# Feed-forward part of a two-layer encoder: product sums accumulated in PSUM, the next chunk's first product moved forward, the middle convolution tap on another engine, and operand preparation of the down-projection ordered behind additions

## The chip, the cores and the metric

The kernel runs on one core of a Trainium2 chip. The metric is the time of one execution on the device, in microseconds (us). The core's engines are named as in the profile: PE multiplies matrices (PEld loads its weights), DVE, ACT and POOL work on vectors, and SP issues most of the DMAs. Each engine works through its own list of instructions in order; semaphores tie the lists together. Matmuls sum in PSUM banks; all other tiles lie in SBUF.

## The reference, cut to what matters

```python
D_MODEL, SEQ, DEPTH, D_FF, CONV_W = 1024, 1024, 2, 2816, 3

def reference(x, ..., ffn_norm, w_up, conv_w, conv_b, w_down):
    for l in range(DEPTH):
        ...
        x = x + mix @ w_out[l]
        hf = rms_norm(x, ffn_norm[l]) @ w_up[l]
        gate, val = hf[..., :D_FF], hf[..., D_FF:]
        gate = depthwise_conv(gate, conv_w[l], conv_b[l])
        x = x + (gelu(gate, approximate=False) * val) @ w_down[l]
    return x
```

The convolution runs over the tokens, with three taps and a bias for each of the 2816 channels. Everything is float32. What stands in the place of the first dots (attention in two forms and a recurrence) is not touched by the change.

## The kernel before

**Tiling.** Activations lie transposed: 128 channels on the partitions, 1024 tokens along the row. The up-projection takes 22 chunks f; a chunk makes 128 channels of the gate and 128 of the value, for all 1024 tokens. Each float32 operand is split in a high and a low part (ACT makes the high one, `split`, L1063; DVE the difference, L1064), and a product is summed from three matmul terms, so a k-step costs three matmuls of 128 by 128 by 512.

**Seven products.** Gate and value, each in two halves of the tokens, form a 2 by 2 block product over two halves of the input channels. It is done in seven block products instead of eight, named "11", "21", "T2", "T3", "T1", "T4" and "22". Each has 12 matmuls (L1114), so a chunk has 84 and a layer 1848. In `up` each product gets a PSUM bank of its own ("pa", "pt" or "pb"), and the shared sums are made on DVE: ACT copies the first product into u2 (L1127), then DVE adds banks into u2, u3, the two halves of g (gate) and of v (value), seven additions of 512 columns (L1121).

**The gate.** `gate` scales g by the row factors rbc of the normalization (POOL, L1154), starts t with the middle tap and the bias (POOL, L1155), adds the two outer taps (DVE, L1156 and L1157), applies gelu (ACT, L1158) and scales by rbc again (POOL, L1159). DVE multiplies t by v (L1144) and SP stores t to the DRAM tensor hid (L1145).

**Weights.** While a chunk's products run, `up_weights` prepares the next chunk's seven weight operands: SP loads rv and rg (L1051 and L1052, 512 KB each), POOL makes four sums of 512 columns in the tiles ws and ws3 (L1059), and each of the seven operands "wo" is split on ACT and DVE. The loads, the sum tile ws and the seven operands take their buffers from one pool of 10 (`NWEIGHT`). A tile that takes a buffer waits for the last user of the tile that held it.

**Down-projection.** Again seven block products, in four groups g = 0 to 3 over 11 steps m, 24 matmuls a step (L1287; some steps 12). `prep` loads a step's pieces (256 KB each), makes sums and differences on DVE and splits them (L1177 is the line of a helper, `tt`, for all of these, and for the additions of `evacuate` too). Two steps are prepared ahead (`DOWN_AHEAD`). The sums of a group stay in PSUM over its 11 steps; at the end of group 0 `evacuate` adds eight banks to the rows X (written X<-X,pa in the profile), and group 1 then takes the same banks.

**Order.** A scheduler lists each engine's instructions ahead of time, from the order in which the code is traced and from its own estimates. `tc.issue_after`, which the change brings in, makes it list what is traced within it behind the named instruction.

Of the kernel before, what the change touches and what calls it, by code (L numbers as in the profile page):

```python
# [12 lines left out]
AF = mybir.ActivationFunctionType  # L13
ALU = mybir.AluOpType
AX = mybir.AxisListType.X

P = 128
D = 1024
T = 1024
# [6 lines left out]
NFF = D_FF // P  # L26
# [67 lines left out]
class Trunk:  # L94
# [953 lines left out]
    def up_weights(self, l, f, eng):  # L1048
        nc = self.nc
        rg, rv = (self.wslot([P, KC, P], name="wraw") for _ in range(2))  # L1050
        nc.sync.dma_start(rv, self.i["w_u"][l, 2 * f + 1])  # L1051
        nc.sync.dma_start(rg, self.i["w_u"][l, 2 * f])  # L1052
        (a11, a12), (a21, a22) = (
            [r.rearrange("p k o -> p (k o)")[:, 512 * j : 512 * j + 512] for j in range(2)] for r in (rv, rg)
        )
        s = self.wslot([P, 2, 512], name="ws")

        def sub(out, a, b, op=ALU.subtract):
            eng.tensor_tensor(out, a, b, op=op)  # L1059

        def split(src):
            o = self.wslot([P, 2, 512], F32R, name="wo")
            nc.scalar.activation(o[:, 0], src, AF.Copy)  # L1063
            nc.vector.tensor_tensor(o[:, 1], src, o[:, 0], op=ALU.subtract)  # L1064
            return o

        yield split(a11)
        yield split(a12)
        sub(s[:, 0], a21, a22, ALU.add)
        sub(s[:, 1], s[:, 0], a11)  # L1070
        yield split(s[:, 1])
        d = self.half([P, 512], "ws3")
        sub(d, a11, a21)
        yield split(d)
        yield split(s[:, 0])
        yield split(a22)
        sub(s[:, 1], a12, s[:, 1])
        yield split(s[:, 1])
# [3 lines left out]

    def up(self, l, X, td, acc, H):
        nc = self.nc
        for name in ("21", "T3", "T1", "T4", "22"):
            for k in range(4):
                a, b, ga, gb = X[k], X[k + 4], self.gain(l, k), self.gain(l, k + 4)
                if name == "21":
                    o = self.split_x(b[:, :512], gb, self.xslot)
                elif name == "22":  # L1090
                    o = self.split_x(b[:, 512:], gb, self.slot)
                elif name == "T1":
                    o = self.split_x(td[k][:, 0], None, self.xslot, nc.gpsimd)
                elif name == "T3":
                    d = self.half([P, 512], "xt")
                    nc.scalar.activation(d, a[:, 512:], AF.Copy, scale=ga)
                    nc.vector.scalar_tensor_tensor(d, b[:, 512:], gb, d, op0=ALU.mult, op1=ALU.subtract)
                    o = self.split_x(d, None, self.xslot)
                else:
                    d = td[k][:, 1]  # L1100
                    nc.vector.scalar_tensor_tensor(d, b[:, :512], gb, d, op0=ALU.mult, op1=ALU.subtract)
                    o = self.split_x(d, None, self.xslot)
                self.B[name, k] = o
        rbc = None
        for f in range(NFF):
            ahead = self.up_weights(l, f + 1, nc.gpsimd) if f + 1 < NFF else iter(())
            ops, self.ops = self.ops, []

            def product(j, x, tag):
                ps = self.bank2([P, 512]) if tag == "pa" else self.bank1([P, 512], tag=tag)  # L1110
                for k in range(4):
                    for u, v in ((0, 0), (0, 1), (1, 0)):
                        st, mv = ops[j][:, u, k * P : (k + 1) * P], self.B[x, k][:, v]
                        nc.tensor.matmul(ps, st, mv, start=k + u + v == 0, stop=k == 3 and u == 1)  # L1114
                o = next(ahead, None)
                if o is not None:
                    self.ops.append(o)
                return ps

            def add(out, x, y):  # L1120
                nc.vector.tensor_tensor(out, x, y, op=ALU.add)  # L1121

            pu = self.slot([P, 2, 512], name="pu")
            u2, u3 = pu[:, 0], pu[:, 1]
            g, v = self.slot([P, T], name="g"), self.slot([P, T], name="v")
            p1 = product(0, "11", "pa")
            nc.scalar.activation(u2, p1, AF.Copy)  # L1127
            p2 = product(1, "21", "pb")
            add(v[:, :512], u2, p2)
            p6 = product(2, "T2", "pt")  # L1130
            add(u2, u2, p6)
            p7 = product(3, "T3", "pt")
            add(u3, u2, p7)
            if rbc is None:
                rbc = self.factors(acc)
            p5 = product(4, "T1", "pb")
            add(g[:, 512:], u3, p5)
            add(u2, u2, p5)
            p4 = product(5, "T4", "pt")
            add(g[:, :512], u3, p4)  # L1140
            p3 = product(6, "22", "pb")
            t = self.gate(l, f, g, rbc)
            add(v[:, 512:], u2, p3)
            nc.vector.tensor_tensor(t, t, v, op=ALU.mult)  # L1144
            nc.sync.dma_start(H[f], t)  # L1145

    def gate(self, l, f, g, rbc):

        nc = self.nc
        cw = PP_CW + (l * NFF + f) * 3  # L1150
        w = [self.pp[:, cw + j : cw + j + 1] for j in range(3)]
        cb = self.pp[:, PP_CB + l * NFF + f : PP_CB + l * NFF + f + 1]
        t = self.slot([P, T], name="t")
        nc.gpsimd.tensor_tensor(g, g, rbc, op=ALU.mult)  # L1154
        nc.gpsimd.tensor_scalar(t, g, w[1], cb, op0=ALU.mult, op1=ALU.add)  # L1155
        nc.vector.scalar_tensor_tensor(t[:, 1:], g[:, : T - 1], w[0], t[:, 1:], op0=ALU.mult, op1=ALU.add)  # L1156
        nc.vector.scalar_tensor_tensor(t[:, : T - 1], g[:, 1:], w[2], t[:, : T - 1], op0=ALU.mult, op1=ALU.add)  # L1157
        nc.scalar.activation(t, t, AF.Gelu)  # L1158
        nc.gpsimd.tensor_tensor(t, t, rbc, op=ALU.mult)  # L1159
        return t  # L1160
# [8 lines left out]
    def down(self, l, H, spill, out):  # L1169

        nc = self.nc
# [4 lines left out]
        def tt(out, a, b, op=ALU.subtract):  # L1176
            nc.vector.tensor_tensor(out, a, b, op=op)  # L1177

        def split2(src):

            hi, lo = (self.xslot([P, 2, 512], F32R, name="bw") for _ in range(2))
            nc.scalar.activation(hi, src, AF.Copy)
            tt(lo, src, hi)
            return (hi[:, 0], lo[:, 0]), (hi[:, 1], lo[:, 1])
# [4 lines left out]
        def prep(g, k, m):  # L1189
# [34 lines left out]
                return ops  # L1224
            return [None, split2(p)]

        def add(x, ps):
            tt(x, x, ps, ALU.add)

        def evacuate(g, j, c, ps):  # L1230
            x, y = X[c], X[4 + c]
# [32 lines left out]
        steps = [(g, k, m) for g in range(4) for m, k in enumerate(DOWN_ORDERS[g])]  # L1264
        ready, late, acc = [], [], [None, None]
        for i, (g, k, m) in enumerate(steps):
            while len(ready) < min(len(steps), i + 1 + DOWN_AHEAD):
                ready.append(prep(*steps[len(ready)]))
            if g < 2:
                residual(g, m)  # L1270
            if m == 0 and g == 0:
                acc[0] = [p[:, h] for p in [self.bank2([P, T]) for _ in range(2)] for h in (h0, h1)]
            if m == 0 and g != 1:
                acc[1] = [self.bank1([P, 512], tag=t) for t in ("pt", "pt", "pb", "pb")]
            late.append((m, ready[i]))
            ready[i] = None
            if n - DOWN_TAIL <= m < n - 1:
                continue
            for j in range(2):
                first = g if j and g > 1 else 0  # L1280
                for c in range(4):
                    for q, ops in late:
                        if ops[j] is None:
                            continue
                        a, b = ops[j]
                        for u, v in ((0, 0), (0, 1), (1, 0)):
                            nc.tensor.matmul(  # L1287
                                acc[j][c],
                                a[u][:, c * P : (c + 1) * P],
                                b[v],  # L1290
                                start=g == first and q + u + v == 0,
                                stop=q == n - 1 and u == 1,
                                skip_group_check=g > first,
                            )
                    if m == n - 1 and ops[j] is not None:
                        evacuate(g, j, c, acc[j][c])
            late = []
        return X

# [169 lines left out]
```

## Time and profile before

| what | value |
|---|---|
| median of 3 runs | 2880.6 us (2879.34 to 2884.51) |
| the profiled execution | 2879.85 us, of which the span is 2878.0 us |
| PE, DVE, ACT, POOL busy | 97%, 78%, 47%, 42% of the span |
| up-projection, layer 0 | 775.87 to 1228.3 us of the span |
| down-projection, layer 0 | 1228.3 to about 1466 us |
| up-projection, layer 1 | 2204.0 to 2654.9 us |
| down-projection, layer 1 | 2654.9 to 2878 us |

A row of a group in the profile names line, engine, operation, the tile written and those read, the shape, the count, the busy time with the mean of one, and the idle time ahead with what ended it. Rows of a timeline begin with the start in us and the length. Matmul rows last longer than the distance between two matmuls, since they overlap; the distance is what counts.

### The profile page before, as it was taken

The page shows a single profiled execution, that of the slowest core. Times are in us where ns is not written, and L with a number is a line of the kernel's source. Part 1 is how long each engine was busy: PE and PEld are TensorE (multiplying, and loading weights), DVE is VectorE, ACT ScalarE, POOL GpSimd, SP SyncE. Part 2 cuts the span into 40 slices and gives each one's busy share as a digit, 9 for nine tenths or more (in the row PEclk, how much of TensorE's full clock was granted, in tenths as well). Part 3 has the DMA queues.
Part 4 walks back from the last instruction along what each step waited for, and adds up shares of the span by engine and source line. Part 5 has one row for each costly group of instructions (what it writes and reads, how often), then busy time and mean ns, then how long its engine had stood idle before and what let it go on. Part 6 is the DMA issues. An engine that isn't in the chain of part 4 may idle for free.

```text
span 2878.0 us, 40091 instructions
## 1 busy us (share of the span) xinstructions
PE 2782.9 (97%) x14984; PEld 2346.7 (82%) x14984; DVE 2253.6 (78%) x3044; ACT 1338.6 (47%) x2273; POOL 1214.2 (42%) x811
## 2 busy tenths in 40 slices
PE   8999999999999999999999999999999999999999
PEld 7999987777878777778899999877777777877787
DVE  5849668897778888896848495788967888888975
ACT  5526367786432222234535264677854222222332
POOL 2516545432366666510015265354323566665000
PEclk9999999999999999999999999999999999999999
DMA  4213262101312222474313033521012222225641
GB/s 148 83 34 101 73 161 70 45 16 46 115 59 87 82 74 87 140 281 140 118 54 85 25 108 85 137 70 45 15 66 95 79 82 74 84 83 196 234 157 66
DMA packets 155202, 273.63 MB, mean 95 GB/s; under 512 B 16768, under 2 KB 74368, under 8 KB 155008
## 3 DMA queue, kind: packets, MB, share of 16 engines
q1 hardware_dynamic: 145216, 241.71, 26.0%
q0 software_dynamic: 9792, 29.36, 3.8%
q8 instruction: 118, 1.93, 0.3%
q14 instruction: 76, 0.62, 0.1%
HBM read 201.80 MB, written 69.21 MB: 94 GB/s over the span
## 4 chain that ended last, share of the span: by engine, by line
PE 56%; DVE 16%; POOL 11%; DMA 7%; issue 6%; ACT 5%; SPq 0%; ACTq 0%; POOLq 0%; DVEq 0%
PE pa L269 10%; PE pa L281 10%; POOL ws L1059 6%; DVE wo L1064 6%; PE pa L1287 6%; DMA wraw<-w_u 5%; PE pb L860 5%; PE pa L774 5%; PE pb L1287 4%; PE pt L1287 4%; PE pt L845 3%; POOL t L1159 3%; ACT wo L1063 2%; PE pt L619 1%; PE pb L619 1%
## 5 line engine op out<-in xcount | busy, mean ns | idle before, releaser
L1114 PE MATMUL pt<-bo,wo 128*128 128x512 f32 x1584 | 392.3, 400 | 30.1 <-DVE pu L1121 24.2
L1114 PEld LDWEIGHTS pt<-bo,wo 128*128 128x128 f32 x1584 | 299.8, 192 | 113.0 <-issue 27.3
L1114 PE MATMUL pb<-bo,wo 128*128 128x512 f32 x1584 | 382.2, 389 | 4.5 <-DVE v L1121 3.9
L1114 PEld LDWEIGHTS pb<-bo,wo 128*128 128x128 f32 x1584 | 296.8, 188 | 67.3 <-ACT t L1158 4.6
L281 PE MATMUL pa<-wh,xh 128*128 128x256 f32 (+1 forms) x864 | 266.1, 308 | 8.3 <-ACT xh L233 8.3
L281 PE MATMUL pa<-wh,xl 128*128 128x256 f32 (+1 forms) x864 | 264.2, 307 | 4.0 <-DVE xl L234 3.9
L281 PE MATMUL pa<-wl,xh 128*128 128x256 f32 (+1 forms) x864 | 264.1, 306 | 1.4 <-DVE wl L336 1.4
L774 PE MATMUL pa<-qk,qk 96*128 96x512 f32 (+1 forms) x896 | 255.1, 411 | 8.6 <-DVE nmb L809 3.2
L1064 DVE TENSOR_TENSOR wo<-ws,wo 128x512 fp32r<-128x512 f32 x176 | 216.2, 1246 | 8.6 <-ACT wo L1063 4.5
L1063 ACT ACTIVATE wo<-ws 128x512 fp32r<-128x512 f32 x176 | 102.0, 624 | 252.2 <-POOL ws L1059 208.5
L855 DVE TENSOR_TENSOR ptl<-pt,pth 128x512 fp32r<-128x512 f32 x240 | 162.0, 684 | 45.5 <-ACT pth L849 44.2
L1287 PE MATMUL pa<-bw,bw 128*128 128x512 f32 x616 | 178.3, 398 | 14.3 <-DVE X L1177 14.3
L774 PEld LDWEIGHTS pa<-qk,qk 96*128 96x128 f32 (+1 forms) x896 | 155.9, 189 | 38.2 <-issue 7.2
L809 DVE CUSTOM_DVE_ANT_0 pb<-pa,toep 128x1024 f32<-128x1024 f32 x128 | 153.6, 1218 | 42.4 <-PE pa L774 39.0
L849 ACT ACTIVATE pth<-pt 128x512 fp32r<-128x512 f32 x256 | 149.0, 597 | 76.2 <-PE pt L845 72.2
L793 POOL TENSOR_SCALAR pa<-pa,z 128x1024 f32<-128x1024 f32 x96 | 110.5, 1151 | 152.9 <-PE pt L845 107.2
L281 PEld LDWEIGHTS pa<-wh,xh 128*128 128x128 f32 x864 | 168.1, 195 | 8.4 <-ACT xh L233 8.3
L281 PEld LDWEIGHTS pa<-wh,xl 128*128 128x128 f32 x864 | 166.9, 194 | 4.7 <-DVE xl L234 4.6
L281 PEld LDWEIGHTS pa<-wl,xh 128*128 128x128 f32 x864 | 168.0, 194 | 1.9 <-DVE wl L336 1.6
L1064 DVE TENSOR_TENSOR wo<-wraw,wo 128x512 fp32r<-128x512 f32 x132 | 151.7, 1152 | 19.4 <-ACT wo L1063 17.2
L812 ACT ACTIVATE pb<-pb,nmb 128x1024 f32<-128x1024 f32 x128 | 147.1, 1151 | 32.2 <-DVE nmb L809 27.2
L1154 POOL TENSOR_TENSOR g<-g,rbc 128x1024 f32<-128x1024 f32 x44 | 108.5, 2466 | 115.8 <-DVE g L1121 115.8
(314 smaller groups left out, 6938.2 us busy)
## 6 DMA issues: line engine op xcount, KB each, us to landing
wraw<-w_u SPq DMA_DIRECT2D x88, 512.0 KB, 4.0
hid<-t SPq DMA_DIRECT2D x44, 512.0 KB, 2.9
dq<-hid SPq DMA_DIRECT2D x66, 256.0 KB, 4.7
bk<-st SPq DMA_DIRECT2D x256, 48.0 KB, 1.7
qk<-bk POOLq DMA_DIRECT2D x32, 384.0 KB, 5.6
da<-w_d SPq DMA_DIRECT2D x44, 256.0 KB, 3.6
dp<-w_d SPq DMA_DIRECT2D x44, 256.0 KB, 4.5
dq<-w_d SPq DMA_DIRECT2D x44, 256.0 KB, 3.4
```

The costliest lines, as they stand in the source:

```text
L269: nc.tensor.matmul(ps[:, hf * 512 : hf * 512 + 512], w, x[:, hf * 512 : hf * 512 + 512], start=first, stop=last)
L281: self.nc.tensor.matmul(ps, x[:, ts], w[:, k % kp, :cols], start=first, stop=last)
L774: nc.tensor.matmul(ps[:, hs], q[:rows, o + t * P : o + (t + 1) * P], kk[w][:rows, hs], start=w == 0, stop=w == 1)
L809: nc.vector.tensor_tensor_reduce(e, ps, self.toep[:, o : o + T], scale=-slope, scalar=3.0e38, op0=ALU.add, op1=ALU.min, accum_out=nm)
L812: nc.scalar.activation(e, e, AF.Exp, bias=nm, scale=-1.0, accum_out=z[:, t, i : i + 1])
L849: nc.scalar.activation(hi[:, kk], ps, AF.Copy)
L855: nc.vector.tensor_tensor(lo[:, kk], ps, hi[:, kk], op=ALU.subtract)
L1059: eng.tensor_tensor(out, a, b, op=op)
L1063: nc.scalar.activation(o[:, 0], src, AF.Copy)
L1064: nc.vector.tensor_tensor(o[:, 1], src, o[:, 0], op=ALU.subtract)
L1114: nc.tensor.matmul(ps, st, mv, start=k + u + v == 0, stop=k == 3 and u == 1)
L1287: nc.tensor.matmul(acc[j][c], a[u][:, c * P : (c + 1) * P], b[v], start=g == first and q + u + v == 0, stop=q == n - 1 and u == 1, skip_gr ...
```

## The change

In `up`, the products T2, T3 and T4 are no longer written to banks of their own: they go on summing in the bank `a` of product 11, and ACT (twice) or DVE reads the bank between them. Product 22 goes on summing in the bank `b` of T1. So the four results need four DVE operations of 512 columns (L1120 of the kernel after; one of them is a multiplication by rbc straight from the bank) and three ACT copies. POOL scales only the half of g that is left (L1153), and the middle tap goes from POOL to ACT (L1170, one activation of 1024 columns with scale and bias). The operands of T1 and T3, and the order of two weight sums, change places. The next chunk's first product is traced ahead of T4 (`begin`). In `down`, each step's preparation is traced under `tc.issue_after` with an addition as its mark: the first steps behind additions of the up-projection's last chunk, those after a group's end behind the fourth and the eighth addition that read its banks.

```diff
--- before.py
+++ after.py
@@ -1069,10 +1069,10 @@
         sub(s[:, 0], a21, a22, ALU.add)
         sub(s[:, 1], s[:, 0], a11)
         yield split(s[:, 1])
+        yield split(s[:, 0])
         d = self.half([P, 512], "ws3")
         sub(d, a11, a21)
         yield split(d)
-        yield split(s[:, 0])
         yield split(a22)
         sub(s[:, 1], a12, s[:, 1])
         yield split(s[:, 1])
@@ -1082,7 +1082,7 @@
 
     def up(self, l, X, td, acc, H):
         nc = self.nc
-        for name in ("21", "T3", "T1", "T4", "22"):
+        for name in ("21", "T1", "T3", "T4", "22"):
             for k in range(4):
                 a, b, ga, gb = X[k], X[k + 4], self.gain(l, k), self.gain(l, k + 4)
                 if name == "21":
@@ -1102,47 +1102,63 @@
                     o = self.split_x(d, None, self.xslot)
                 self.B[name, k] = o
         rbc = None
+
+        def product(j, x, ps, first=True):
+
+            for k in range(4):
+                for u, v in ((0, 0), (0, 1), (1, 0)):
+                    st, mv = self.ops[j][:, u, k * P : (k + 1) * P], self.B[x, k][:, v]
+                    nc.tensor.matmul(
+                        ps, st, mv, start=first and k + u + v == 0, stop=k == 3 and u == 1, skip_group_check=not first
+                    )
+            self.ops[j] = None
+            o = next(self.ahead, None)
+            if o is not None:
+                self.ops.append(o)
+
+        def add(out, x, y, op=ALU.add):
+            return nc.vector.tensor_tensor(out, x, y, op=op)
+
+        def begin():
+
+            v, a = self.slot([P, T], name="v"), self.bank2([P, 512])
+            product(0, "11", a)
+            nc.scalar.activation(v[:, :512], a, AF.Copy)
+            return v, a
+
+        self.ahead = iter(())
+        v, a = begin()
         for f in range(NFF):
-            ahead = self.up_weights(l, f + 1, nc.gpsimd) if f + 1 < NFF else iter(())
-            ops, self.ops = self.ops, []
-
-            def product(j, x, tag):
-                ps = self.bank2([P, 512]) if tag == "pa" else self.bank1([P, 512], tag=tag)
-                for k in range(4):
-                    for u, v in ((0, 0), (0, 1), (1, 0)):
-                        st, mv = ops[j][:, u, k * P : (k + 1) * P], self.B[x, k][:, v]
-                        nc.tensor.matmul(ps, st, mv, start=k + u + v == 0, stop=k == 3 and u == 1)
-                o = next(ahead, None)
-                if o is not None:
-                    self.ops.append(o)
-                return ps
-
-            def add(out, x, y):
-                nc.vector.tensor_tensor(out, x, y, op=ALU.add)
-
-            pu = self.slot([P, 2, 512], name="pu")
-            u2, u3 = pu[:, 0], pu[:, 1]
-            g, v = self.slot([P, T], name="g"), self.slot([P, T], name="v")
-            p1 = product(0, "11", "pa")
-            nc.scalar.activation(u2, p1, AF.Copy)
-            p2 = product(1, "21", "pb")
-            add(v[:, :512], u2, p2)
-            p6 = product(2, "T2", "pt")
-            add(u2, u2, p6)
-            p7 = product(3, "T3", "pt")
-            add(u3, u2, p7)
+            last = f + 1 == NFF
+            self.ahead = self.up_weights(l, f + 1, nc.gpsimd) if not last else iter(())
+            g, c = self.slot([P, T], name="g"), self.bank1([P, 512], tag="pt")
+            product(1, "21", c)
+            self.mark = [add(v[:, :512], v[:, :512], c)]
+
+            product(2, "T2", a, False)
+            nc.scalar.activation(v[:, 512:], a, AF.Copy)
             if rbc is None:
                 rbc = self.factors(acc)
-            p5 = product(4, "T1", "pb")
-            add(g[:, 512:], u3, p5)
-            add(u2, u2, p5)
-            p4 = product(5, "T4", "pt")
-            add(g[:, :512], u3, p4)
-            p3 = product(6, "22", "pb")
+            b = self.bank1([P, 512])
+            product(3, "T1", b)
+
+            product(4, "T3", a, False)
+            nc.scalar.activation(g[:, 512:], a, AF.Copy)
+            self.mark.append(add(g[:, 512:], g[:, 512:], b))
+            ops, self.ops = self.ops[:7], self.ops[7:]
+            coming = None if last else begin()
+            self.ops = ops + self.ops
+            product(5, "T4", a, False)
+            add(g[:, :512], a, rbc[:, :512], ALU.mult)
+            nc.gpsimd.tensor_tensor(g[:, 512:], g[:, 512:], rbc[:, 512:], op=ALU.mult)
+            product(6, "22", b, False)
             t = self.gate(l, f, g, rbc)
-            add(v[:, 512:], u2, p3)
+            add(v[:, 512:], v[:, 512:], b)
             nc.vector.tensor_tensor(t, t, v, op=ALU.mult)
             nc.sync.dma_start(H[f], t)
+            self.ops = self.ops[7:]
+            if not last:
+                v, a = coming
 
     def gate(self, l, f, g, rbc):
 
@@ -1151,8 +1167,7 @@
         w = [self.pp[:, cw + j : cw + j + 1] for j in range(3)]
         cb = self.pp[:, PP_CB + l * NFF + f : PP_CB + l * NFF + f + 1]
         t = self.slot([P, T], name="t")
-        nc.gpsimd.tensor_tensor(g, g, rbc, op=ALU.mult)
-        nc.gpsimd.tensor_scalar(t, g, w[1], cb, op0=ALU.mult, op1=ALU.add)
+        nc.scalar.activation(t, g, AF.Identity, bias=cb, scale=w[1])
         nc.vector.scalar_tensor_tensor(t[:, 1:], g[:, : T - 1], w[0], t[:, 1:], op0=ALU.mult, op1=ALU.add)
         nc.vector.scalar_tensor_tensor(t[:, : T - 1], g[:, 1:], w[2], t[:, : T - 1], op0=ALU.mult, op1=ALU.add)
         nc.scalar.activation(t, t, AF.Gelu)
@@ -1224,8 +1239,11 @@
                 return ops
             return [None, split2(p)]
 
+        marks = []
+
         def add(x, ps):
-            tt(x, x, ps, ALU.add)
+            nonlocal marks
+            marks.append(nc.vector.tensor_tensor(x, x, ps, op=ALU.add))
 
         def evacuate(g, j, c, ps):
             x, y = X[c], X[4 + c]
@@ -1265,7 +1283,11 @@
         ready, late, acc = [], [], [None, None]
         for i, (g, k, m) in enumerate(steps):
             while len(ready) < min(len(steps), i + 1 + DOWN_AHEAD):
-                ready.append(prep(*steps[len(ready)]))
+
+                with self.tc.issue_after(self.mark[0].ins):
+                    ready.append(prep(*steps[len(ready)]))
+                if len(self.mark) > 1:
+                    self.mark.pop(0)
             if g < 2:
                 residual(g, m)
             if m == 0 and g == 0:
@@ -1294,6 +1316,8 @@
                             )
                     if m == n - 1 and ops[j] is not None:
                         evacuate(g, j, c, acc[j][c])
+            if marks:
+                self.mark, marks = [marks[3], marks[7]] if len(marks) == 8 else marks[3:], []
             late = []
         return X
 
```

On DVE, in a chunk in the middle of the up-projection, there stood before (wo is a weight operand's low part, pu holds u2 and u3, t is the gate's tile):

```order
L1121 TENSOR_TENSOR pu_1577_9267<-pu_1577_9267,pb_1592_9347 128x512
L1064 TENSOR_TENSOR wo_1593_9360<-ws_1583_9287,wo_1593_9360 128x512
L1064 TENSOR_TENSOR wo_1595_9378<-wraw_1581_9283,wo_1595_9378 128x512
L1121 TENSOR_TENSOR g_1578_9268<-pu_1577_9267,pt_1594_9365 128x512
L1064 TENSOR_TENSOR wo_1597_9396<-ws_1583_9287,wo_1597_9396 128x512
L1121 TENSOR_TENSOR v_1579_9269<-pu_1577_9267,pb_1596_9382 128x512
L1064 TENSOR_TENSOR wo_1606_9430<-wraw_1604_9426,wo_1606_9430 128x512
L1156 SCALAR_TENSOR_TENSOR t_1598_9399<-g_1578_9268,pp_88,t_1598_9399 128x1023
L1157 SCALAR_TENSOR_TENSOR t_1598_9399<-g_1578_9268,pp_88,t_1598_9399 128x1023
L1064 TENSOR_TENSOR wo_1608_9447<-wraw_1604_9426,wo_1608_9447 128x512
```

and now, from the first operand that needs a freshly loaded rv to the chunk's last operand:

```order
L1064 TENSOR_TENSOR wo_1556_9383<-wraw_1554_9379,wo_1556_9383 128x512
L1064 TENSOR_TENSOR wo_1557_9399<-wraw_1554_9379,wo_1557_9399 128x512
L1120 TENSOR_TENSOR g_1534_9228<-pa_1528_9167,rbc_1385_8030 128x512
L1171 SCALAR_TENSOR_TENSOR t_1550_9355<-g_1534_9228,pp_88,t_1550_9355 128x1023
L1120 TENSOR_TENSOR v_1527_9166<-v_1527_9166,pb_1541_9267 128x512
L1064 TENSOR_TENSOR wo_1559_9418<-ws_1555_9382,wo_1559_9418 128x512
L1172 SCALAR_TENSOR_TENSOR t_1550_9355<-g_1534_9228,pp_88,t_1550_9355 128x1023
L1064 TENSOR_TENSOR wo_1560_9433<-ws_1555_9382,wo_1560_9433 128x512
L1064 TENSOR_TENSOR wo_1564_9454<-ws3_1563_9452,wo_1564_9454 128x512
L1064 TENSOR_TENSOR wo_1565_9470<-wraw_1553_9378,wo_1565_9470 128x512
L1157 TENSOR_TENSOR t_1550_9355<-t_1550_9355,v_1527_9166 128x1024
L1064 TENSOR_TENSOR wo_1566_9488<-ws_1555_9382,wo_1566_9488 128x512
```

The outer taps (before L1156 and L1157, now L1171 and L1172) moved apart, and the product t times v (now L1157) stands ahead of the operand from ws that is the chunk's last.

On POOL a chunk had these rows before:

```order
L1154 TENSOR_TENSOR g_1600_9410<-g_1600_9410,rbc_1391_8056 128x1024
L1155 TENSOR_SCALAR t_1620_9541<-g_1600_9410,pp_88 128x1024
L1059 TENSOR_TENSOR ws3_1634_9625<-wraw_1626_9568,wraw_1625_9567 128x512
L1059 TENSOR_TENSOR ws_1627_9571<-wraw_1625_9567 128x512
L1159 TENSOR_TENSOR t_1620_9541<-t_1620_9541,rbc_1391_8056 128x1024
L1059 TENSOR_TENSOR ws_1627_9571<-ws_1627_9571,wraw_1626_9568 128x512
L1059 TENSOR_TENSOR ws_1627_9571<-wraw_1626_9568,ws_1627_9571 128x512
```

and has these now:

```order
L1153 TENSOR_TENSOR g_1585_9636<-g_1585_9636,rbc_1385_8030 128x512
L1059 TENSOR_TENSOR ws3_1614_9860<-wraw_1605_9787,wraw_1604_9786 128x512
L1059 TENSOR_TENSOR ws_1606_9790<-wraw_1604_9786 128x512
L1059 TENSOR_TENSOR ws_1606_9790<-ws_1606_9790,wraw_1605_9787 128x512
L1059 TENSOR_TENSOR ws_1606_9790<-wraw_1605_9787,ws_1606_9790 128x512
L1174 TENSOR_TENSOR t_1601_9763<-t_1601_9763,rbc_1385_8030 128x1024
```

The middle tap is gone, the first scaling is half as long, and the second scaling of t now comes behind all four weight sums instead of between them.

The buffers changed hands too. Before, SP's load of rg (L1052) took the buffer that the previous chunk's ws had held, and so waited for that chunk's last low part on DVE (L1064, wo<-ws); the load of rv (L1051), for which SP's list has its place behind the store of t, took a buffer that had come free earlier. Now the load of rv takes the buffer of ws and waits for that low part, and the load of rg stands behind rv on SP. SP's order itself (rg, store, rv) is as it was.

On DVE at the end of group 0 of the down-projection, there stood before (dp, dq and dw are pieces being prepared; X<-X,pa is an addition that frees a bank):

```order
L1177 TENSOR_TENSOR dp_11430<-dq_11431,dp_11430 128x1024
L1177 TENSOR_TENSOR dq_11209<-da_11674,dp_11208 128x512
L1177 TENSOR_TENSOR dq_11251<-da_11711,dp_11250 128x512
L1177 TENSOR_TENSOR dp_11476<-dq_11477,dp_11476 128x1024
L1177 TENSOR_TENSOR X_11310<-X_11310,pa_11136 128x512
L1177 TENSOR_TENSOR X_11356<-X_11356,pa_11137 128x512
```

and now:

```order
L1246 TENSOR_TENSOR X_11179<-X_11179,pa_11004 128x512
L1246 TENSOR_TENSOR X_11225<-X_11225,pa_11005 128x512
L1192 TENSOR_TENSOR dp_10986<-dq_10987,dp_10986 128x1024
L1246 TENSOR_TENSOR X_11317<-X_11317,pb_11009 128x512
L1192 TENSOR_TENSOR dp_11034<-dq_11035,dp_11034 128x1024
L1192 TENSOR_TENSOR dp_11076<-dq_11077,dp_11076 128x1024
L1192 TENSOR_TENSOR dp_11118<-dq_11119,dp_11118 128x1024
```

The additions moved ahead of the differences of the steps m = 2 and later of group 1, nine rows of 1024 columns, one of which stands between the last additions and eight behind them.

## The prediction

> **What bounds the kernel now.** I read the page's groups first, then the totals of PE's waits, then a window in the middle of the up-projection, and last the chain of waits there.
>
> ```profile
> L1114 PE MATMUL pt<-bo,wo 128*128 128x512 f32 x1584 | 392.3, 400 | 30.1 <-DVE pu L1121 24.2
> PE pt L1114 <- DVE pu L1121: 24.2, 38, 3.7
> PE pa L1287 <- DVE X L1177: 14.3, 2, 7.1
> 920.29:1116.76 196.47, 193.08 (x841) 156.89 (x841) 172.02 (x170) 55.38 (x90) 124.15 (x71) 1.00 0.25 81
> 1041.02 2.88 PE L1114 MATMUL pb<-bo,wo 128*128 128x512 f32 x12
> 1043.74 2.88 PE L1114 MATMUL pa<-bo,wo 128*128 128x512 f32 x12
> 1046.46 2.88 PE L1114 MATMUL pb<-bo,wo 128*128 128x512 f32 x12
> L1064 DVE TENSOR_TENSOR wo<-ws,wo x84: 677/680/2939, 799.8 to 1204.7; 128x512 fp32r<-128x512 f32 x84
> ```
>
> The fourth row is a window of ten chunks: its length, the busy time of PE, PEld, DVE, ACT and POOL, then the granted clock (1.00), the DMA share and GB/s. A chunk takes 196.47 / 10 = 19.65 us. PE's rows of 12 matmuls start 2.72 us apart, so 84 matmuls need 7 x 2.72 = 19.04 us. PE could run only 0.61 us a chunk faster, although it is busy nearly all the time; what holds it to 19.65 is elsewhere. The waits for pu are 38 short ones, and two more, of 7.1 us, stand in the down-projection. The last row gives the marks I use below: the last chunk's last low part starts at 1204.7 and takes up to 2.94, so it ends near 1207.6; 18 chunks earlier it is 1207.6 - 18 x 19.65 = 853.9.
>
> The chain in that window, in order of time (start, length, what):
>
> ```profile
> 988.58 2.95 DVE wo L1064
> 991.58 3.62 DMA wraw<-w_u
> 995.33 3.17 POOL ws L1059 x2
> 998.51 2.36 POOL t L1159
> 1000.93 2.19 issue
> 1003.12 0.68 DVE pu L1121
> 1003.79 0.61 DVE wo L1064
> 1004.47 1.70 POOL ws L1059
> 1006.19 0.64 ACT wo L1063
> 1006.86 0.70 DVE wo L1064
> 1007.58 0.64 ACT wo L1063
> 1008.25 2.94 DVE wo L1064
> ```
>
> It is a **ring**: the last low part of one chunk's weights frees a buffer, a load follows, sums and splits follow, and 1008.25 - 988.58 = 19.67 us later the same place comes again. PE isn't in it. So the time of a chunk is the longer of the ring and PE's 19.04 us.
>
> The long pieces of the ring are waits between DVE and POOL:
>
> ```profile
> 988.56 2.40 POOL L1154 TENSOR_TENSOR g<-g,rbc 128x1024 f32<-128x1024 f32 x1 [2.07 <-DVE g L1121]
> 988.58 2.93 DVE L1064 TENSOR_TENSOR wo<-ws,wo 128x512 fp32r<-128x512 f32 x1
> 991.44 0.68 DVE L1121 TENSOR_TENSOR v<-pu,pb 128x512 f32<-128x512 f32 x1
> 996.77 1.74 POOL L1059 TENSOR_TENSOR ws<-wraw 128x512 f32<-128x512 f32 x1
> L1059 POOL TENSOR_TENSOR ws<-ws,wraw 128x512 f32<-128x512 f32 x10 | 12.9, 1288 | 0.0
> ```
>
> The low part, 680 ns as a rule, took 2.93 us beside a POOL instruction of 2.40 us. POOL's sum takes 1.29 us alone and 1.74 with a low part ahead of it. The addition from PSUM stays at 0.68. The Trainium skill (SBUF — State Buffer, Who interferes with whom) states the rule: a DVE instruction with two SBUF inputs and a GpSimd instruction that reads SBUF lock each other out, and the loser blocks fully. By that rule the pieces after the load add up in the new ring too; without it they would overlap, and my first rival below would hold. The trace agrees with it: 0.60 + 2.40 gives the 2.93.
>
> **The up-projection, part by part.** DVE loses three additions a chunk, POOL the middle tap and half a scaling, and both POOL pieces that held DVE in the ring go. ACT gains the tap and two copies; it is busy 5.5 us of a chunk, so I cost these at nothing except where they stand in a chain. What counts is the new ring. The load that now waits for the last low part is rv, and rg queues behind it, with the store of t just ahead.
>
> ```profile
> 2255.24 0.33 SPq L1145 DMA_DIRECT2D hid<-t  x1
> 2255.89 0.33 SPq L1051 DMA_DIRECT2D wraw<-w_u  x1
> 2256.50 0.37 SPq L1052 DMA_DIRECT2D wraw<-w_u  x1
> DMA to landing us min/median/max: 5.2/5.2/5.2
> 2231.67 0.33 SPq L1051 DMA_DIRECT2D wraw<-w_u  x1
> 2232.19 0.33 SPq L1052 DMA_DIRECT2D wraw<-w_u  x1
> DMA to landing us min/median/max: 4.4/4.4/4.4
> L1156 DVE SCALAR_TENSOR_TENSOR t<-g,pp,t x44: 1270/1272/2301, 814.6 to 2661.3; 128x1023 f32<-128x1023 f32 x44
> L1159 POOL TENSOR_TENSOR t<-t,rbc x44: 2361/2383/3377, 821.2 to 2665.1; 128x1024 f32<-128x1024 f32 x44
> L1144 DVE TENSOR_TENSOR t<-t,v x44: 1210/2294/2305, 826.5 to 2670.6; 128x1024 f32<-128x1024 f32 x44
> ```
>
> At 2255.24 the three DMAs happen to stand together: rg lands 0.61 + 5.2 = 5.8 us after the issue of rv (the first landing line is that of the rg at 2256.50). Without a store it is 0.52 + 4.4 = 4.9 (second pair and line). Before, the ring had rg alone, 3.62.
>
> From the order of the instructions I lay the ring by hand, taking DVE and POOL in turn. Landing, with 0.1 to start: 5.9. Then POOL's four sums, 4 x 1.29 = 5.2; between them and behind them, on DVE, five low parts at 0.60 from start to start (3.0), two outer taps at 1.2 (2.4), an addition for v (0.6); then t times rbc on POOL, 2.4; t times v, 1.2; the last low part, 0.7. The sum is 21.4. The tap on ACT (about 1.1, like gelu) lies beside a POOL sum, gelu beside the fourth. With the landing of 4.9 it is 20.4; a further collision like that of 1.74 instead of 1.29 would give 21.9. I take **21.0**, nearer to the row with the store, since the store is there, less a little for the turns that may fall well. PE then pauses 21.0 - 19.04 = 2 us a chunk, in two places: at product 11 for DVE's reading of the bank (g), and at T4 for ACT's copy of g, which stands behind the last operand's high part.
>
> Chunks 1 to 3 have their loads early, before buffers run short, so their turns are shorter. I place the third's mark at 849 (853.9 before), an estimate good to about 4 us. Then 18 turns: 849 + 18 x 21.0 = 1227.0. Behind the last mark six products are left, T4 and 22 of chunk 20 and four of chunk 21: 72 matmuls, 6 x 2.72 = 16.3, and some 3.5 of waits where DVE also prepares the down-projection's first operands. The end is 1246.8.
>
> ```profile
> 1216.42 0.93 PE L1114 MATMUL pb<-bo,wo 128*128 128x512 f32 x3 [1.78 <-DVE v L1121]
> 1221.06 5.14 PE L1114 MATMUL pt<-bo,wo 128*128 128x512 f32 x12 [3.71 <-DVE pu L1121]
> 1226.04 2.24 PE L1114 MATMUL pb<-bo,wo 128*128 128x512 f32 x9
> 841.42 3.02 PE L1114 MATMUL pt<-bo,wo 128*128 128x512 f32 x12 [2.46 <-DVE pu L1121]
> ```
>
> Before, PE's last row of the phase started at 1226.04 and ended at 1228.3, with two pauses and 12 matmuls at half pace. So a layer's up-projection is **18.5 us longer**, 37.0 for both. A pause of 3.71 left the next 12 matmuls slow (5.14), one of 2.46 didn't (3.02); the new pauses are shorter than that, and I add nothing for the clock.
>
> **The down-projection.** At the end of group 0, PE waits for the first addition to free a bank, which DVE had listed behind differences for later steps:
>
> ```profile
> 1288.53 1.22 DVE L1177 TENSOR_TENSOR dp<-dq,dp 128x1024 f32<-128x1024 f32 x1
> 1292.01 1.27 DVE L1177 TENSOR_TENSOR X<-X,pa 128x512 f32<-128x512 f32 x2
> 1292.74 5.13 PE L1287 MATMUL pa<-bw,bw 128*128 128x512 f32 x12 [7.14 <-DVE X L1177]
> 1297.71 0.39 PE L1287 MATMUL pt<-bw 128*128 128x512 f32 x1
> ```
>
> The loss is 7.14 and 1297.71 - 1292.74 - 2.72 = 2.25 of slow matmuls, 9.4 us. Now the additions come first. What is late next are the nine differences: 9 x 1.14 (their distance) = 10.3, then a difference, a split and a low part, about 13 after group 0's last matmul. Two steps are ready, 48 matmuls or 10.9 us. PE pauses about 2 us (0 to 4) instead, and a layer gains 7.4; **14.8 for both**. At the later group ends I see no stall before and none now. SP's loads of these steps go out early enough either way: the pieces of step 2 are in hand by then.
>
> **Sum.** 37.0 - 14.8 = +22.2 on 2879.85, the profiled execution's own time, which is 0.75 under the median of 2880.6. I say 2902.
>
> **Rivals.** *PE becomes the bound (faster).* If DVE and POOL overlap more than I lay it, the ring falls under 19.04 and the matmuls decide: with 0.2 for restarts, 849 + 18 x 19.25 + 19.8 = 1215.3, 13.0 less a layer; 26.0 and 14.8 give 2839. For it speaks that POOL drops from 12.4 us a chunk by the window's row to some 8.9, and DVE by three additions. Against it, the load that has grown by over 2 us in a ring that PE isn't in. Of 16 us behind the landing, 2.4 or more would have to overlap; it decides from there.
>
> *The load lands early.* A ring of 20.2 gives 4.1 a layer, 8.2 - 14.8: 2873. For it speaks the landing of 4.9 without a store; against it, the store issued within 0.7 us in every chunk. This is also the case in which the change saves DVE work that nobody waited for.
>
> *The held preparation costs what it saves.* If the first operands behind the marks come 7 us later than I lay them, PE's pause stays as long as it was, and nothing is gained in the down-projection: 2917. For it speaks that DVE must then do at the boundary what it did ahead of it; against it, two ready steps.
>
> **How the numbers follow.** My forecast with rings of 20.5 to 21.5, 2884 to 2920: 0.47. PE the bound: 0.22. An early landing, 2865 to 2884: 0.19. The held preparation: 0.12. A measurement of this kernel can tell about 0.2%, 5.8 us, from no change. Faster by that takes the 0.22 and half of the early landing: 0.32. Within it: the other half and the forecast's low edge, 0.13. Slower: 0.55. A tenth of a microsecond in the ring is 3.6 us of time, so the range is wide: 2846 to 2924, which cuts the PE-bound case and the top of the last.
>
> **What would show it.** In the window of ten chunks the period should be near 21.0; the chain should show rv and rg (about 5.8 us from the last low part), four POOL sums, t, t times v. PE's waits should name the g copy on ACT (bank pa) and g on DVE, near 1 us each. At the first group end of the down-projection PE should wait about 2 us for a low part, and no 12 matmuls at half pace. A period of 19.3 with PE's rows back to back would make me wrong on the ring, and one over 22 on the landing.

## The result, and the profile after

The changed kernel takes **2905.77 us** (median of 4 runs, 2904.39 to 2909.03); the kernel before took 2879.97 beside it (4 runs). The ratio is 1.0088, with a 95% interval of 1.0071 to 1.0106: slower by 0.9%. The profiled execution has a span of 2904.4 us against 2878.0, so 26.4 more. 2902 was forecast.

The costliest group of the up-projection's matmuls, the largest of PE's waits, and two windows of ten chunks each, one in each layer (length, then busy time of PE, PEld, DVE, ACT and POOL, granted clock, DMA share, GB/s):

```profile
L1111 PE MATMUL pa<-bo,wo 128*128 128x512 f32 x2112 | 511.7, 393 | 52.0 <-ACT g L1146 46.5
PE pa L1111 <- ACT g L1146: 46.5, 38, 1.5
912.17:1119.65 207.48, 194.78 (x844) 156.95 (x842) 139.01 (x141) 78.57 (x120) 114.34 (x60) 1.00 0.23 77
2391.60:2601.28 209.68, 195.03 (x840) 156.30 (x840) 139.55 (x142) 78.56 (x120) 113.58 (x60) 1.00 0.22 76
```

A chunk takes 20.75 us in layer 0 and 20.97 in layer 1, where it took 19.65. DVE is busy 13.9 us of it instead of 17.2, POOL 11.4 instead of 12.4: both engines have less to do, and the chunk is longer. PE waits once a chunk for ACT's copy of g, up to 1.5 us, and after that copy it runs at its pace.

The chain of waits over one turn (start, length, what):

```profile
1016.83 0.69 DVE wo L1064
...
1017.66 0.33 SPq L1051
...
1018.09 5.42 DMA wraw<-w_u
...
1023.64 3.05 POOL ws L1059 x2
1026.69 0.07 issue
1026.76 2.16 POOL ws L1059
1028.93 0.02 issue
1028.95 0.64 ACT wo L1063
1029.59 0.02 issue
1029.62 0.70 DVE wo L1064
1030.32 0.07 issue
1030.39 2.28 POOL ws L1059
...
1032.69 0.64 ACT wo L1063
...
1033.39 2.55 issue
1035.94 0.68 DVE wo L1064
1036.62 0.73 DVE t L1157
```

Behind the last low part, which ends at 1017.52, SP issues both loads; rg lands at 1018.09 + 5.42 = 1023.51, 6.0 us later. Before, rg landed 3.7 us behind the low part (988.58 + 2.95 to 991.58 + 3.62). Then the four weight sums take 1.79 to 2.28 us where DVE is ahead of them and 1.3 where not; one low part is held 2.55 us while POOL scales t (POOL's row of that runs from 1032.73 to 1035.47). It is the same ring as before with a longer load in it and a little less behind the load: from the low part's end to the first sum it took 3.8 us and takes 6.1; all that follows took 19.65 - 3.8 = 15.8 and takes 20.75 - 6.1 = 14.6. The landing is 2.3 us longer, and what follows it, with less work on DVE and POOL, 1.2 shorter.

The loads on SP's queue, and the first addition's place at the end of group 0 in the down-projection:

```profile
1016.93 0.33 SPq L1158 DMA_DIRECT2D hid<-t  x1
1017.66 0.33 SPq L1051 DMA_DIRECT2D wraw<-w_u  x1
1018.09 0.48 SPq L1052 DMA_DIRECT2D wraw<-w_u  x1
1309.03 9.16 DVE L1192 TENSOR_TENSOR dp<-dq,dp 128x1024 f32<-128x1024 f32 x8
1319.98 0.73 PE L1309 MATMUL pt<-bw 128*128 128x512 f32 x2 [1.55 <-ACT bw L1197]
```

The store stands right ahead of the two loads. DVE does eight of the nine differences in one stretch, after the additions, and PE waits 1.55 us for the operand behind them, where it waited 7.14 for a bank.

### The profile page after: what moved, and what is told of

It reads as the page before. It is cut to its first block, busy times and chain, and to the rows that moved or that the text cites. A ratio compares the mean times of both kernels' runs of the same rounds, so it can differ in the third digit from the quotient of the medians.

```text
span 2904.4 us, 40019 instructions
## 1 busy us (share of the span) xinstructions
PE 2779.4 (96%) x14984; PEld 2339.3 (81%) x14984; DVE 2106.8 (73%) x2912; ACT 1438.2 (50%) x2405; POOL 1164.9 (40%) x767
## 4 chain that ended last, share of the span: by engine, by line
PE 53%; DVE 13%; POOL 12%; DMA 9%; issue 7%; ACT 5%; SPq 1%; ACTq 0%; POOLq 0%; DVEq 0%
PE pa L269 10%; POOL ws L1059 9%; PE pa L281 8%; DMA wraw<-w_u 7%; PE pa L1309 6%; PE pb L860 5%; PE pa L774 5%; PE pt L1309 4%; PE pb L1309 4%; DVE wo L1064 3%; PE pt L845 3%; ACT wo L1063 2%; PE pt L619 1%; PE pb L619 1%; PE pt L281 1%
## 5 line engine op out<-in xcount | busy, mean ns | idle before, releaser
L1111 PE MATMUL pa<-bo,wo 128*128 128x512 f32 x2112 | 511.7, 393 | 52.0 <-ACT g L1146 46.5
L1111 PEld LDWEIGHTS pa<-bo,wo 128*128 128x128 f32 x2112 | 392.1, 188 | 156.5 <-ACT g L1146 63.7
L1064 DVE TENSOR_TENSOR wo<-ws,wo 128x512 fp32r<-128x512 f32 x176 | 246.6, 1404 | 59.5 <-ACT wo L1063 55.2
L1111 PE MATMUL pb<-bo,wo 128*128 128x512 f32 x1056 | 253.6, 389 | 0.0
L1111 PEld LDWEIGHTS pb<-bo,wo 128*128 128x128 f32 x1056 | 198.2, 188 | 41.2
L1063 ACT ACTIVATE wo<-ws 128x512 fp32r<-128x512 f32 x176 | 110.0, 629 | 220.4 <-DVE wo L1064 110.0
L1064 DVE TENSOR_TENSOR wo<-wraw,wo 128x512 fp32r<-128x512 f32 x132 | 98.3, 770 | 164.3 <-ACT wo L1063 164.3
L1063 ACT ACTIVATE wo<-wraw 128x512 fp32r<-128x512 f32 x132 | 78.4, 622 | 224.1 <-DMA wraw<-w_u 196.3
```

The lines of the kernel that those rows point to most:

```text
L1111: nc.tensor.matmul(ps, st, mv, start=first and k + u + v == 0, stop=k == 3 and u == 1, skip_group_check=not first)
```

## The experiments

Each run is compared with the kernel before on the same chip; the before's median was 2880.9 to 2881.1 us in all three sets.

### The parts alone

`up_only` leaves the hold out:

```diff
-                with self.tc.issue_after(self.mark[0].ins):
-                    ready.append(prep(*steps[len(ready)]))
-                if len(self.mark) > 1:
-                    self.mark.pop(0)
+                ready.append(prep(*steps[len(ready)]))
```

> The up-projection as changed, the down-projection's preparation in its old order. Both theories of the longer chunk (a load more in the ring, or the new order on DVE and POOL) leave the period at 20.8 to 21.0 us. The pause of 7.1 us and the slow matmuls at the end of group 0 come back, 9.4 instead of 1.9 us a layer: 2905.8 + 15 = 2921 us. A rival, in which holding the preparation has moved the cost to the start of the down-projection, gives 2906 to 2913.

2910.16 us, ratio 1.0106 (1.0091 to 1.0121). The period stayed (20.7 and 20.9 us on average over 18 turns), so the longer chunk belongs to the up-projection's edits. But the hold was worth less here than I expected: 4.4 us between the medians, 3.5 with each taken against the kernel before beside it. The intervals of the two ratios overlap, so the times alone don't tell it from nothing. In the profiled executions the pieces from the up-projection's last low part to the end of the down-projection, where the hold acts, are 3.8 and 5.5 us longer without it. PE's wait at the end of group 0 is shorter in this kernel than in the one before:

```profile
1308.90 3.48 PE L1306 MATMUL pa<-bw,bw 128*128 128x512 f32 x8 [4.09 <-DVE X L1246]
```

4.09 us, not 7.14. Why DVE reaches the additions sooner wasn't tried.

`down_only` gives the kernel before the marks and the hold, and nothing else:

```diff
-            add(v[:, :512], u2, p2)
+            self.mark = [add(v[:, :512], u2, p2)]
...
-            add(g[:, 512:], u3, p5)
+            self.mark.append(add(g[:, 512:], u3, p5))
...
-                ready.append(prep(*steps[len(ready)]))
+                with self.tc.issue_after(self.mark[0].ins):
+                    ready.append(prep(*steps[len(ready)]))
+                if len(self.mark) > 1:
+                    self.mark.pop(0)
```

> The up-projection as before, with marks on the same two sums, and the down-projection's preparation held behind them. Period 19.65 as before. If the hold saves what the pause cost: 2880 - 15 = 2865 us. If it moves the cost to the start of the down-projection or into the later groups: 2875 to 2880.

2868.3 us, ratio 0.9954 (0.9937 to 0.9971): 12.6 us gained, most of the 15. The hold is a gain of its own, and it was covered by the other part of the change.

### The loads and the ring

`rv_off_ring` gives the weights one buffer more, so that rv no longer takes the buffer of the sums ws:

```diff
-NSLOT = 13
+NSLOT = 12
...
-NWEIGHT = 10
+NWEIGHT = 11
```

> The changed kernel with 11 buffers in the pool of the weights (and one fewer, 12, in the pool of g, v and t), so that the load of rv waits for the first low part instead of the last and only rg is left on the ring. If the load is what lengthened the ring: rg alone lands in about 3.6 instead of 5.8 us, the ring would be 20.8 - 2.2 = 18.6, less than the 19.04 of the matmuls, so the period is 19.1 to 19.4 and the time 2906 - 2 x 18 x 1.5 = 2850 us (2840 to 2860). If the order on DVE and POOL lengthened it, the period stays at 20.8 and the time at 2905.

2857.61 us, ratio 0.9923 (0.9908 to 0.9938). Two of SP's loads and the window of ten chunks:

```profile
1003.80 0.33 SPq L1052 DMA_DIRECT2D wraw<-w_u  x1
1014.37 0.33 SPq L1051 DMA_DIRECT2D wraw<-w_u  x1
906.59:1100.88 194.29, 193.18 (x841) 156.92 (x840) 127.19 (x141) 76.28 (x120) 87.70 (x60) 1.00 0.24 82
```

rv is now issued 10.6 us behind rg, for the chunk after; only rg is left behind the last low part. The period is 19.43 us, 1.3 shorter, with every instruction on DVE and POOL as it was in kind and number, though not in order. POOL's scaling of g, which lay beside the landing in the changed kernel, now stands between the sums:

```profile
1007.58 1.29 POOL L1059 TENSOR_TENSOR ws<-wraw,wraw 128x512 f32<-128x512 f32 x1 [4.40 <-DMA wraw<-w_u]
1008.83 1.29 POOL L1153 TENSOR_TENSOR g<-g,rbc 128x512 f32<-128x512 f32 x1
```

The last low part ends at 1003.73, so it takes 3.85 us to the first sum instead of 6.1, and all that follows takes 15.6 instead of 14.6. The shorter landing gained 2.3 us, and the pieces behind it, in their new order, took 1.0 more. So the load that came into the ring made the chunk longer. I had expected 19.1 to 19.4.

`ws_elsewhere` reaches for the same thing in another way, with ws in the pool that holds g, v and t:

```diff
-        s = self.wslot([P, 2, 512], name="ws")
+        s = self.slot([P, 2, 512], name="ws")
```

> The changed kernel with the sum tile ws in the pool of g, v and t. The load of rv then waits for the last but one low part, the store of t follows, and rg stands behind the store and no longer waits for the last low part. If the loads are what counts: rg is issued about 1.2 us earlier than now, so the period is near 19.6 (19.2 to 20.0) and the time about 2862 us. If the order on DVE and POOL counts: 20.8 and 2905.

2838.7 us, ratio 0.9852 (0.9834 to 0.987), better than expected. In the window of layer 1 and on SP's queue there:

```profile
2344.60:2534.97 190.37, 190.37 (x842) 157.68 (x841) 134.84 (x141) 78.56 (x121) 104.33 (x60) 1.00 0.27 83
2444.90 0.33 SPq L1051 DMA_DIRECT2D wraw<-w_u  x1
2446.64 0.33 SPq L1158 DMA_DIRECT2D hid<-t  x1
2447.06 0.38 SPq L1052 DMA_DIRECT2D wraw<-w_u  x1
```

PE is busy all 190.37 us: 19.04 a chunk, the pace of the matmuls. rv goes out 1.74 us ahead of the store instead of behind it, and rg no longer waits for the last low part. In layer 0 the 18 turns average 19.35 us. DVE's order moved in this run too (the second outer tap ahead of the low parts from ws, the last low part ahead of t times v), so the run by itself doesn't part the loads from the order. This kernel is faster than the kernel before and than the changed one.

`before_ws_elsewhere` makes the same edit in the kernel before.

> The kernel before with the sum tile ws in the pool of g, v and t, the edit that made the changed kernel fast. Here the load of rv waits for the last but one low part and rg follows it directly. If the loads alone set the pace, the chunk reaches the matmuls' 19.04 to 19.2 and the time 2880 - 36 x 0.5 = 2862 us. If the turns of DVE and POOL (about 11 us of POOL and 7.7 us of DVE operations with two SBUF inputs a chunk, 18.7 together) hold it as well, it stays at 19.4 to 19.7: 2870 to 2881.

2954.1 us, ratio 1.025 (1.0233 to 1.0267). Neither guess: it is 73 us slower. The window and the loads say why:

```profile
995.04:1212.00 216.96, 199.72 (x839) 160.01 (x838) 174.91 (x171) 54.12 (x90) 125.45 (x70) 0.97 0.20 73
1021.49 0.33 SPq L1051 DMA_DIRECT2D wraw<-w_u  x1
1021.92 0.37 SPq L1052 DMA_DIRECT2D wraw<-w_u  x1
```

In this kernel the edit moves rv the wrong way. It was issued well before rg; now it waits for a low part late in the chunk (it ends at 1021.47), and rg follows directly. So both loads are in the ring, and the period is 21.7 us against 19.65. That is the change's own trouble made in the other kernel, by one line and without any sum in PSUM. But from the low part's end to the first sum it takes 4.8 us (1021.47 to 1026.30) where it took 3.8, so the load is 1.0 of the 2.05. The other half lies in the pieces behind it, whose order on DVE and POOL moved too.

`before_ws_and_hold` adds the hold to that.

> The same with the down-projection's preparation held as in the changed kernel: 12.6 us less than the run before it (2850 to 2868), as the hold alone gave. What is left to 2838.7 is what the sums in PSUM, the first product's place and the tap on ACT are worth once the loads are off the ring.

2942.8 us, 11.3 less than without it; the hold again brings its 11 to 13. Since the loads stayed in the ring, the difference to 2838.7 doesn't give the worth of the sums in PSUM; that stays open.

`both_loads_early` joins the edits of `rv_off_ring` and `ws_elsewhere` in the changed kernel.

> Both edits together: ws in the other pool, 11 buffers for the weights and 12 there. The load of rv waits for the first low part, that of rg for the last but one, and SP issues rg ahead of the store. If the matmuls already set the pace with ws elsewhere (19.04 a chunk in layer 1), only the few us of waits in layer 0 are left to gain: 2832 to 2839 us. If the smaller pool of g, v, t and ws makes those wait: 2845 to 2860.

2836.2 us, ratio 0.9837 (0.9822 to 0.9853). The interval lies over that of `ws_elsewhere`, so the two aren't told apart, though this run's marks are 19.04 us apart through nearly all of both layers. With PE at its pace the loads have nothing more to give.

### The turns of DVE and POOL

`tap_on_pool` is the changed kernel with the middle tap back on POOL:

```diff
-        nc.scalar.activation(t, g, AF.Identity, bias=cb, scale=w[1])
+        nc.gpsimd.tensor_scalar(t, g, w[1], cb, op0=ALU.mult, op1=ALU.add)
```

> The changed kernel with the middle tap back on POOL, between two weight sums; all else as changed. If DVE and POOL take turns in the ring, a POOL instruction of 1.2 to 1.5 us more adds itself to the ring in place of an activation that lay beside a sum: period 20.8 + 1.3 = 22.1, time 2906 + 36 x 1.3 = 2953 us (2935 to 2965). If POOL has room (it is busy less than half of a chunk), the period and the 2906 us stay.

2944.3 us, ratio 1.0222 (1.0207 to 1.0238). The window and a piece of the chain:

```profile
978.49:1198.09 219.60, 199.68 (x840) 159.79 (x840) 131.59 (x141) 66.11 (x110) 108.11 (x70) 0.98 0.21 72
1009.68 1.30 POOL ws L1059
1010.98 1.19 POOL t L1170
1012.19 2.30 DVE t L1171
```

The period is 21.96, by 1.2 more, about the length of the tap (1.19) that now stands in the chain. POOL is busy 108 of 220 us, under half, and still one more instruction on it cost its whole length here. It isn't so piece by piece: the outer tap behind it takes 2.30 us, beside a sum on POOL, instead of 1.52 in the changed kernel's turn above, while the four sums take 6.1 us together instead of 7.5.

`ws_elsewhere_tap_pool` moves the tap back in the kernel that has ws in the other pool.

> The changed kernel with ws in the other pool and the middle tap on POOL. Here SP issues rg ahead of the store. POOL and DVE have 18.0 us of operations that lock each other out in a chunk; with the loads off the ring they could just fit in 19.04: 2839 to 2850 us. If the tap on ACT is what lets the matmuls set the pace: a period of 19.6 to 20 and 2860 to 2875.

2882.83 us, ratio 1.0007 (0.9998 to 1.0016); 20.3 us a chunk by its window. It came out beyond the slower of my two cases. The chain of waits in one turn has this:

```profile
1028.74 4.64 DMA wraw<-w_u
...
1034.88 1.29 POOL g L1153
...
1036.26 1.21 POOL t L1170
```

The load of rg is still in the chain, with POOL's scaling and tap behind it. So this run doesn't show the turns of DVE and POOL alone holding the chunk above the matmuls' 19.04; the load and they do it together. In this kernel the tap on ACT is worth 44 us.

### What the hold is worth where PE sets the pace

`ws_elsewhere_no_hold` is `ws_elsewhere` with the edit of `up_only`.

> The changed kernel with ws in the other pool and the down-projection's preparation in its old order. If the hold is worth what it saved alone in the kernel before (12.6 us): 2838.7 + 12.6 = 2851 us. If the up-projection's changes already shorten the pause at the end of group 0, as the run without the hold suggests (4.1 instead of 7.1 us there, 4.4 us in all): 2843 us.

2853.64 us, ratio 0.9898 (0.9881 to 0.9914), 15 us over the run with the hold, which is the size of the larger case. It isn't a clean figure: the profiled executions differ by 22.2 us, of which 10.0 are the 18 turns of layer 1 (19.6 us each instead of 19.04) and 5.5 and 4.7 the pieces behind the two last low parts, where the hold acts. Why the turns are slower wasn't tried.

## Why the prediction was right

**The bound.** The step that carried it, that the chunk is the longer of the ring and PE's 19.04 us and that rv's load comes into the ring, was right, and two runs show it from both sides: rv out of the ring takes 1.3 us off the changed kernel's chunk, with 2.3 less for the landing, and both loads behind one late low part bring the other kernel to 21.7, with 1.0 more for it. The rest of the changes in both comes with the order on DVE and POOL, which each edit also moved; no run holds that order fixed.

**The ring's terms.** The landing was laid at 5.9 with its start; measured from the low part's end to the first sum it is 1023.64 - 1017.52 = 6.1. All that follows was laid at 15.5 and shaded to 15.1; 20.75 - 6.1 = 14.6 in layer 0. The ring was put at 21.0 and is 20.75 and 20.97. The turns of DVE and POOL held: `tap_on_pool` gave 1.2 us more where 1.2 to 1.5 were expected of one more POOL instruction in the chain.

**PE's pauses.** One of two came out. The wait at T4 for ACT's copy is there (1.5); the one at product 11 for DVE's reading of the bank is nearly absent from the window, 2.0 us in 17 chunks. The sum of both, 2 us a chunk, was near: the period less 19.04 is 1.7 to 1.9.

**The phases.** From the marks of the last low parts and PE's first and last matmuls, in us:

| piece | forecast | layer 0 | layer 1 |
|---|---|---|---|
| start of the up-projection to the third mark | -4.9 | -5.1 | -4.1 |
| 18 turns | +24.4 | +20.4 | +24.4 |
| last mark to the end of the down-projection | -8.3 | -7.2 | -7.0 |
| sum | +11.2 | +8.0 | +13.3 |

The forecast for the last row is 19.8 - 20.7 at the phase's end and -7.4 at the end of group 0. The -7.4 came out (1.55 us of waiting and a slow first matmul for 7.14 and slow matmuls), but it isn't all the hold's: without the hold the wait there is already down to 4.09. At the end of the phase some 3.5 us of waits were laid; PE's waits from the last mark to the first steps of the down-projection are 1.60, 0.69, 0.29 and 1.18, so 3.8 in layer 0, and 4.3 in layer 1. Where the rest of the 1.1 and 1.3 in the last row lies isn't shown. The first row holds a pause that the prediction doesn't have: in each layer's first chunk PE waits 5.63 us for a low part, and the 10 matmuls behind it take 4.64.

**What was luck.** The layers' pieces add to 21.3 us, and 22.2 were forecast; layer 0's turns, 4.0 under the forecast, are in part made up for by the last rows, 1.1 and 1.3 over theirs. The split between the two parts of the change came out less well. The forecast has 37.0 for the up-projection and -14.8 for the hold. With the hold left out the change costs 29.3 us, and the hold takes 3.5 off that, where in the kernel before it takes 12.6 off: the parts don't add. One reason is the wait of 4.09 instead of 7.14 at the end of group 0; the rest stays open. The other 5 of the 26.4 lie outside of what I had priced: 3.0 ahead of the first up-projection and 2 between and behind the layers. Over all the runs that first start stood anywhere from 773.6 to 782.4 us, in kernels whose text ahead of it is alike, so it is no effect of these edits that I could name.

**The rivals.** The PE-bound case, 2839, isn't what this change does, but with ws elsewhere the kernel comes to it, at 2838.7. It gets there with its loads issued earlier and DVE's order moved, so not by the overlap of DVE and POOL alone, which this rival goes by. In the changed kernel what follows the load in the ring did get shorter, by 1.2 us, but the load's new buffer cost 2.3. The early landing (2873) fell with the store ahead of both loads, and the held preparation gave back little over 1 us a layer, not 7.

## What to carry to other kernels

Where tiles of several kinds share one pool, a change of order decides which tile's buffer a load inherits, and with that what it waits for: read it from the list of instructions before counting work saved. An engine's share of busy time says little when it takes turns with another; count the instructions of both that stand in the chain. And a part that gains may be covered by one that loses, so time the parts alone, and don't expect their gains to add.

## What the runs showed of the hardware

A pause of PE of 2.0 to 2.5 us may or may not leave the next matmuls slow. With the same wait, first in `tap_on_pool`, eight chunks apart, then in `before_ws_elsewhere`, in neighbouring chunks:

```profile
1023.34 4.62 PE L1111 MATMUL pa<-bo,wo 128*128 128x512 f32 x12 [2.50 <-ACT g L1146]
1199.29 3.03 PE L1111 MATMUL pa<-bo,wo 128*128 128x512 f32 x12 [2.53 <-ACT g L1146]
1035.99 2.97 PE L1114 MATMUL pt<-bo,wo 128*128 128x512 f32 x12 [2.02 <-DVE pu L1121]
1057.79 4.58 PE L1114 MATMUL pt<-bo,wo 128*128 128x512 f32 x12 [2.06 <-DVE pu L1121]
```

In each pair one group of 12 matmuls took 1.6 us longer than the other. The prediction had read from one row of 2.46 us that such a pause costs nothing, which these rows don't bear out. In the middle of the changed kernel's up-projection the pauses are 1.5 us at most, and the 12 matmuls behind them take about 3.0 us, as at full pace. In the windows of `before_ws_elsewhere` and `tap_on_pool`, with periods near 22 us, the granted clock fell to 0.97 and 0.98.
